# A modulation vector's sums over the partitions, 512 columns at once or four times 128

## The chip, the cores and the metric

The kernel runs on one core of a Trainium2 chip. The metric is the device time of one execution in microseconds; the number for a version is the median of its runs. Engines are named as in the profile: PE does matmuls (PEld loads their weights), DVE and ACT do elementwise work, POOL (GpSimd) issues DMAs and a few operations of its own, SP issues DMAs only.

## What is computed

Two layers of a backbone over 512 latent tokens and 256 context tokens, with 1024 features and in float32. A layer is a SwiGLU feed-forward part (FFN), a token mixer (a gMLP in layer 0, attention in layer 1) and a second FFN. Each of these six parts is modulated by three vectors, a shift, a scale and a gate, that come from a conditioning vector:

```python
def modulation(cond, w_mod, b_mod):
    m = jax.nn.silu(cond) @ w_mod + b_mod
    return jnp.split(m[..., None, :], N_MOD, axis=-1)

def ffn_sublayer(x, shift, scale, gate, w_in, w_out, ln_g, ln_b):
    y = swiglu(modulate(x, shift, scale), w_in, w_out)
    return layer_norm(ALPHA * x + 0.5 * gate * y, ln_g, ln_b)
...
        m_lat = modulation(c, w_mod[i], b_mod[i])
        m_ctx = modulation(c_ctx, w_mod[i], b_mod[i])
```

There are two conditionings, one for the latent tokens and one for the context, and nine vectors of 1024 per layer. The products of `silu(cond)` with `w_mod` (1024 x 9216 per layer) are what this case is about.

## The kernel before

Each float32 operand of a matmul is split into a high part (a cast on ACT) and a low part (a subtraction on DVE), and each product is made of three matmuls. So ACT and DVE prepare every tile of weights (`raw`, loaded by SP, becomes `w`) and every tile of activations that PE uses.

An FFN has two phases. The in-projection multiplies by the first weight matrix (in a form with fewer products, with sums and differences of weight tiles on DVE) and stores most of the resulting activations in DRAM: `act<-stage`, a DMA that POOL issues (line 90 is a helper that issues for many). The out-projection then goes twice over 22 pieces of activations, once per half of 512 output columns. In step x it multiplies piece x for six blocks of 128 tokens, 18 matmuls, while piece x+3 is prepared: POOL issues the load `q<-act` from DRAM (two DMAs of 384 columns per piece, into six buffers `q`), ACT casts `acts<-q`, DVE makes the low part `acts<-q,acts`. At the change of halves DVE takes the six finished banks out of PSUM (`q<-ps,gate`), which must have begun before PE can reuse the first.

The modulation vectors are made beside all this, without PE. `mod_unit` (lines 453 to 483) makes one vector in two halves of 512 columns. For each half it goes over eight blocks of 128 rows of `w_mod`: SP loads a block into `mraw` (three buffers), and DVE multiplies it by the conditioning's value of each row and adds it to `acc`, once per conditioning (two for all vectors up to (1, 4), one after that). After eight blocks each of the 128 partitions of `acc` holds a partial result for each of the 512 columns. Line 476 sums over the partitions, on POOL, with the result in every partition, and line 477 adds partition 0 to the vector in DRAM (`mod`, where the bias stands already) by a DMA that POOL issues too. Two of the 18 vectors are made by PE at the start, and 16 are left to this code: 12 with two conditionings and 4 with one, in two halves each, which makes 56 sums.

The units are cut into steps by `yield`; `fill` and `fill_pair` take the next step in slots that the phases offer. DVE, ACT, PE, SP and the DMAs of POOL keep the order in which the program was written in these phases (the class `Pinned`). Line 476 calls POOL directly and not through `Pinned`, so a scheduler may place the sums. Each engine works its own queue in order, so that what stands behind a sum in POOL's queue waits for it.

Of the kernel before, what the change touches and what calls it, by code (L numbers as in the profile page):

```python
# [13 lines left out]
P = 128  # L14
# [80 lines left out]
class Backbone:  # L95
# [357 lines left out]
    def mod_unit(self, l, i):  # L453

        nc, io = self.nc, self.io
        nconds = self.nconds(l, i)
        m = self.mods[l, i] = self.dram.tile([2, D], F32, name=f"mod{l}{i}")
        for c in range(nconds):
            self.pool.dma_start(m[c : c + 1, :], io["b_mod"][l, i * D : i * D + D].unsqueeze(0))
        for half in range(2):  # L460
            accs = [self.acc() for _ in range(nconds)]
            for k in range(KD):
                raw, dve = self.next_raw(), self.dve
                self.light = nconds == 1
                for c in range(nconds):
                    cs = self.cs[:, c * KD + k : c * KD + k + 1]
                    if k:
                        dve.scalar_tensor_tensor(accs[c], raw, cs, accs[c], ALU.mult, ALU.add)
                    else:
                        dve.tensor_scalar(accs[c], raw, cs, None, ALU.mult)  # L470
                self.filler_raw()
                if k < KD - 1:
                    yield
            s = slice(half * 512, half * 512 + 512)
            for c in range(nconds):
                nc.gpsimd.partition_all_reduce(accs[c], accs[c], P, bass_isa.ReduceOp.add)  # L476
                nc.gpsimd.dma_start(m[c : c + 1, s], accs[c][0:1, :], accum_op=ALU.add)
            yield
        self.mod_sent.add((l, i))
        if i % 3 == 2:  # L480
            self.mod_done.add((l, i))
        elif {(l, i - i % 3), (l, i - i % 3 + 1)} <= self.mod_sent:
            self.later(READ_LATER, lambda: self.mod_columns(l, i - i % 3))
# [1870 lines left out]
```

## Time and profile before

| | |
|---|---|
| median of 3 runs | 2781.74 us (2780.76 to 2783.99) |
| the profiled execution | 2782.34 us |
| its span in the profile | 2780.6 us |
| mean clock granted to PE | 0.996 of full speed |
| idle time of PE in the span | 51.8 us |
| sums of line 476: count, busy time | 56, 206.6 us |
| DMAs of line 477: count, busy time on POOL | 56, 46.9 us |
| `q<-act` loads: count of DMAs, busy time on POOL | 234, 132.2 us |
| read from and written to HBM | 383.40 and 64.19 MB |

An engine's share of the span is its busy time, whatever it waits for next. POOL's busy time for a sum runs from its issue, so it includes what a sum waits for once it has been issued. In the chain of waits each row is what the next one waited for last. A DMA's row on POOL is the issue; the transfer comes after it. A group's name reads out<-in; `x2` at the end of a timeline's row is two instructions merged into it.

### The profile page before, as it was taken

Reading aid. Unit: us, or ns where it says so; the run is one execution under the profiler, and the core shown is the slowest. Engines: PE = TensorE matmul, PEld = TensorE weight load, DVE = VectorE, ACT = ScalarE, POOL = GpSimd, SP = SyncE. Lnnn points to the kernel's source line nnn. Section 1 sums busy time; section 2 is a strip of 40 time slices with the busy share of each in tenths; the row PEclk is TensorE's granted clock in tenths of the full one; section 3 lists DMA queues with packets and bytes.
Section 4 is the critical chain, followed back from the end, with each engine's and each line's share of the span. In section 5 each row is a group of like instructions: output and inputs, shape, how many; then the busy total and the mean of one; then the engine's idle time right before and its main releaser. Section 6 shows DMA issues by size and latency. Waiting matters only on the chain.

```text
span 2780.6 us, 40722 instructions
## 1 busy us (share of the span) xinstructions
PE 2728.8 (98%) x14234; PEld 2460.8 (89%) x14234; DVE 2082.2 (75%) x3554; ACT 1314.7 (47%) x2624; POOL 554.4 (20%) x627
## 2 busy tenths in 40 slices
PE   7999999999999999999999999999999999999998
PEld 5999987888899988899998889999888888888887
DVE  6879989587789876687998659789795698733445
ACT  6644432475666632554444246444432666623321
POOL 1003144212122233100314120013242121000001
PEclk9999999999999999999999999999999999999999
DMA  7444566367656674344547434445594424354352
GB/s 235 133 140 139 147 221 220 104 212 234 199 180 196 191 265 146 114 149 142 143 139 240 158 107 145 144 143 145 179 304 144 144 76 100 125 149 132 109 169 87
DMA packets 408134, 448.09 MB, mean 161 GB/s; under 512 B 29624, under 2 KB 289144, under 8 KB 407928
## 3 DMA queue, kind: packets, MB, share of 16 engines
q1 hardware_dynamic: 371416, 331.99, 38.3%
q0 software_dynamic: 36512, 113.51, 13.4%
q8 instruction: 111, 1.82, 0.3%
q14 instruction: 95, 0.78, 0.1%
HBM read 383.40 MB, written 64.19 MB: 161 GB/s over the span
## 4 chain that ended last, share of the span: by engine, by line
PE 77%; DVE 7%; issue 5%; DMA 4%; ACT 4%; POOL 2%; SPq 0%; DVEq 0%; ACTq 0%; POOLq 0%
PE ps L90 77%; DVE w L90 1%; DMA mraw<-in_w_mod_dram 1%; DVE acc L90 1%; POOL acc L476 1%; PE pp L90 1%; ACT w L90 1%; DMA raw<-in_w_mod_dram 1%; DMA q<-act 1%; DMA acc<-in_gmlp_w_in_dram 1%; DMA raw<-in_gmlp_w_in_dram 1%; ACT h L694 1%; ACT z L2252 0%; POOL q L90 0%; DVE z L90 0%
## 5 line engine op out<-in xcount | busy, mean ns | idle before, releaser
L90 PE MATMUL ps<-comb,w 128*128 128x384 f32 x6552 | 1153.6, 336 | 6.5 <-DVE w L90 2.5
L90 PEld LDWEIGHTS ps<-comb,w 128*128 128x128 f32 x6552 | 1139.1, 189 | 10.1 <-DVE w L90 3.8
L90 PE MATMUL ps<-w,acts 128*128 128x512 f32 (+1 forms) x3792 | 861.6, 389 | 5.3 <-DVE q L90 4.8
L90 PEld LDWEIGHTS ps<-w,acts 128*128 128x128 f32 x3792 | 707.2, 188 | 151.6 <-DVE q L90 6.1
L90 ACT CAST w<-raw 128x512 fp32r<-128x512 f32 x643 | 397.5, 621 | 627.7 <-PE ps L90 535.3
L90 DVE TENSOR_TENSOR w<-raw,w 128x512 fp32r<-128x512 f32 x643 | 474.7, 743 | 283.1 <-ACT w L90 281.7
L90 DVE SCALAR_TENSOR_TENSOR acc<-mraw,cs,acc 128x512 f32<-128x512 f32 x392 | 279.1, 745 | 24.7 <-DMA mraw<-in_w_mod_dram 24.5
L476 POOL PARTITION_ALL_REDUCE acc<-acc x56 | 206.6, 3697 | 324.3 <-DVE acc L90 297.1
L90 PE MATMUL ps<-h,w 128*128 128x512 f32 (+1 forms) x1152 | 241.4, 372 | 0.2 <-DVE w L174 0.2
L90 PEld LDWEIGHTS ps<-h,w 128*128 128x128 f32 x1152 | 203.3, 188 | 37.7 <-DVE w L174 0.4
L90 POOL DMA_DIRECT2D act<-stage x86 | 48.5, 564 | 902.5 <-DVE stage L90 840.1
L90 ACT COPY q<-ps 128x384 f32<-128x384 f32 (+1 forms) x218 | 104.3, 481 | 238.0 <-PE ps L90 237.9
L90 POOL DMA_DIRECT2D q<-act x234 | 132.2, 601 | 419.5 <-DVE acts L90 278.6
L90 DVE TENSOR_TENSOR w<-sums,w 128x512 fp32r<-128x512 f32 x234 | 165.1, 712 | 45.3 <-ACT w L90 45.1
L90 PE MATMUL ps<-w,comb 128*128 128x512 f32 x756 | 173.7, 391 | 0.5 <-DVE w L90 0.2
L90 PEld LDWEIGHTS ps<-w,comb 128*128 128x128 f32 x756 | 141.4, 188 | 31.5 <-DVE w L90 1.0
L90 ACT CAST w<-sums 128x512 fp32r<-128x512 f32 x234 | 145.1, 621 | 50.9 <-DVE sums L355 29.3
L90 ACT CAST acts<-q 128x384 fp32r<-128x384 f32 (+1 forms) x272 | 132.1, 519 | 73.9 <-DMA q<-act 55.2
L90 DVE TENSOR_TENSOR acts<-q,acts 128x384 fp32r<-128x384 f32 (+1 forms) x272 | 153.6, 602 | 11.1 <-ACT acts L90 11.0
L204 POOL TENSOR_TENSOR rs<-ve,mhalf 128x1 f32<-128x1 f32 (+3 forms) x47 | 38.6, 820 | 274.5 <-DVE ve L201 170.7
L90 DVE TENSOR_TENSOR q<-q,ps 128x384 f32<-128x384 f32 (+1 forms) x81 | 46.2, 570 | 57.9 <-PE ps L90 57.9
L174 DVE TENSOR_TENSOR w<-raw,w 128x512 fp32r<-128x512 f32 x101 | 67.2, 689 | 26.7 <-ACT w L173 26.2
(203 smaller groups left out, 2485.6 us busy)
## 6 DMA issues: line engine op xcount, KB each, us to landing
raw<-in_ffn_w_in_dram SPq DMA_DIRECT2D x400, 256.0 KB
mraw<-in_w_mod_dram SPq DMA_DIRECT2D x256, 256.0 KB
raw<-in_ffn_w_out_dram SPq DMA_DIRECT2D x176, 256.0 KB
q<-act POOLq DMA_DIRECT2D x224, 192.0 KB, 4.3
raw<-in_gmlp_w_in_dram SPq DMA_DIRECT2D x132, 256.0 KB
act<-stage POOLq DMA_DIRECT2D x76, 384.0 KB, 3.2
zhat<-z POOLq DMA_DIRECT2D x26, 512.0 KB, 3.0
raw<-in_gmlp_w_out_dram SPq DMA_DIRECT2D x48, 256.0 KB
```

The lines of the kernel that those rows point to most:

```text
L90: return self.tc.keep_in_program_order(f(*args, **kwargs))
L174: self.lows.append((key, lambda: self.dve.tensor_tensor(lo, src, hi.bitcast(F32), ALU.subtract)))
L204: self.last_rstd = self.nc.gpsimd.tensor_tensor(rs, ve, self.mhalf[:, 0:1].to_broadcast([P, n]), ALU.pow).ins
L476: nc.gpsimd.partition_all_reduce(accs[c], accs[c], P, bass_isa.ReduceOp.add)
L694: self.act.activation(h32[:, kk], ps[:, s], AF.Identity, bias=bi, scale=sc)
```

## The change

The sum of 512 columns becomes four sums of 128 columns, one after another on POOL, over consecutive parts of the same tile. The DMA to `mod` behind them is as before and takes all 512 columns.

```diff
             for c in range(nconds):
-                nc.gpsimd.partition_all_reduce(accs[c], accs[c], P, bass_isa.ReduceOp.add)
+                for x in range(4):
+                    part = accs[c][:, x * P : x * P + P]
+                    nc.gpsimd.partition_all_reduce(part, part, P, bass_isa.ReduceOp.add)
                 nc.gpsimd.dma_start(m[c : c + 1, s], accs[c][0:1, :], accum_op=ALU.add)
```

The order of the instructions of PE, DVE, ACT and SP is the same in both kernels. On POOL the 56 sums become 224. The rows of POOL's queue in the first half of the first out-projection, before (a DMA `q<-act_7` loads stored piece 7; `mod_3862` is vector 4 of layer 0; an `ISA` row with `acc` is a sum, line 476 before and 478 now):

```order
L90 DMA q<-act_5_969 128x384 x2
L90 DMA q<-act_6_970 128x384 x2
L476 ISA acc<-acc 128x512
L477 DMA mod_3862<-acc 16x1x32
L476 ISA acc<-acc 128x512
L477 DMA mod_3862<-acc 16x1x32
L90 DMA q<-act_7_971 128x384 x2
L90 DMA q<-act_8_972 128x384 x2
```

And now, at the same place:

```order
L90 DMA q<-act_5_969 128x384 x2
L90 DMA q<-act_6_970 128x384 x2
L478 ISA acc<-acc 128x128 x4
L479 DMA mod_3886<-acc 16x1x32
L478 ISA acc<-acc 128x128 x4
L479 DMA mod_3886<-acc 16x1x32
L90 DMA q<-act_7_971 128x384 x2
L90 DMA q<-act_8_972 128x384 x2
```

The loads of pieces 7 and 8 stand behind eight short sums instead of two long ones; nothing else has moved. In the in-projections and in the gMLP both sums of a pair stood ahead of both DMAs at some places. One of them, in the gMLP, before:

```order
L90 DMA act_13_7176<-stage 128x768
L476 ISA acc<-acc 128x512 x2
L477 DMA mod_7638<-acc 16x1x32 x2
L90 DMA mod_8691<-in_b_mod_dram 16x64 x2
L90 DMA act_14_7177<-stage 128x768
```

And now:

```order
L90 DMA act_13_7224<-stage 128x768
L478 ISA acc<-acc 128x128 x5
L479 DMA mod_7686<-acc 16x1x32
L478 ISA acc<-acc 128x128 x3
L479 DMA mod_7686<-acc 16x1x32
L90 DMA mod_8751<-in_b_mod_dram 16x64 x2
L90 DMA act_14_7225<-stage 128x768
```

Here the first conditioning's DMA now stands behind the fifth short sum, ahead of the last three of the second conditioning. There are five such places.

## The prediction

> **What bounds the kernel now.** I read the busy shares first, then a table of stretches, then what PE waits for.
>
> ```profile
> PE 2728.8 (98%) x14234; PEld 2460.8 (89%) x14234; DVE 2082.2 (75%) x3554; ACT 1314.7 (47%) x2624; POOL 554.4 (20%) x627
> ```
>
> PE is busy in 98% of the span, so all that anything else can give back is 52 us, and POOL, where the change is, works a fifth of the time. An edit on POOL costs or gains only where POOL's lateness, or what POOL takes from DVE, reaches PE. The table of stretches says where PE is not full: the columns are length, busy time with count for PE, PEld, DVE, ACT and POOL, granted clock, DMA share, GB/s.
>
> ```profile
> 60.00:360.00 300.00, 298.72 (x1726) 298.05 (x1727) 254.51 (x413) 152.03 (x305) 37.76 (x34) 1.00 0.47 138
> 360.00:470.00 110.00, 108.08 (x495) 91.19 (x494) 97.37 (x141) 38.28 (x76) 58.54 (x56) 1.00 0.70 240
> 1500.00:1590.00 90.00, 90.00 (x398) 74.28 (x397) 64.33 (x107) 26.11 (x52) 23.00 (x31) 1.00 0.60 201
> 1980.00:2090.00 110.00, 107.11 (x485) 89.44 (x484) 91.19 (x148) 39.23 (x76) 42.76 (x49) 1.00 0.84 280
> ```
>
> The first row is an FFN's in-projection: sums run there too, yet PE idles 1.3 us in 300, and not for them. The second and fourth are first halves of out-projections, with DVE at 89% and 83% of their 110 us; the third is such a half with DVE at 71% and no idle PE at all. The table of PE's waits, asked of 360 to 470 us, of 2080 to 2090, and of 870 to 890 in the gMLP (two rows), gives:
>
> ```profile
> PE ps L90 <- DVE q L90: 1.9, 1, 1.9
> PE ps L90 <- DVE q L90: 0.3, 1, 0.3
> PE ps L90 <- DVE q L90: 1.7, 1, 1.7
> PE ps L90 <- DVE S L90: 0.4, 1, 0.4
> ```
>
> Small sums, but a PE that waits for DVE has no reserve left: whatever makes DVE later before that point is paid in full. The chain of waits (start, length, what) back from PE's 1.9 us wait, which ended at 467.10, is this:
>
> ```profile
> 412.36 4.44 DMA q<-act
> 428.61 5.21 POOL acc L476
> 434.93 3.21 POOL acc L476
> 441.70 4.09 DMA q<-act
> 466.36 0.69 DVE q L90
> 467.10 3.02 PE ps L90 x12
> ```
>
> The sums (line 476) stand in it, and behind each pair the load of the next stored activations, `q<-act`. POOL's own timeline at the pair before (start, length, instruction) shows why:
>
> ```profile
> 400.44 1.08 POOL L90 DMA_DIRECT2D q<-act  x2 [11.27 <-DVE acts L90]
> 401.56 5.02 POOL L476 PARTITION_ALL_REDUCE acc<-acc  x1
> 406.87 0.83 POOL L477 DMA_DIRECT2D mod<-acc  x1 [0.30 <-POOL acc L476]
> 407.48 3.45 POOL L476 PARTITION_ALL_REDUCE acc<-acc  x1
> 411.22 0.80 POOL L477 DMA_DIRECT2D mod<-acc  x1 [0.30 <-POOL acc L476]
> 411.77 1.93 POOL L90 DMA_DIRECT2D q<-act  x3
> ```
>
> POOL issues no load from 401.5 to 411.8, because two sums and their two DMAs stand ahead in its queue. ACT, DVE and PE need those activations in turn. **So the first half of the first out-projection (360 to 470 us) is where a longer sum costs time.**
>
> **The change part by part.** Removed are 56 sums of 512 columns, added 224 of 128; no other engine's order changes, and no new wait stands anywhere but POOL.
>
> *One piece.* What a sum takes, by the groups of the page and by the answer for its line (min/median/max in ns):
>
> ```profile
> L476 POOL PARTITION_ALL_REDUCE acc<-acc x56 | 206.6, 3697 | 324.3 <-DVE acc L90 297.1
> L476 POOL PARTITION_ALL_REDUCE acc<-acc x56: 3223/3473/5366, 221.2 to 2598.4; - x56
> ```
>
> 3.22 us is one sum with nothing in its way; the mean is 0.47 us longer. No sum of another width is in the trace, so the fixed part F of the 3.22 us is bounded from both sides. With F, four pieces take 3.22 + 3F. Near the low end stand POOL's other instructions:
>
> ```profile
> L90 POOL TENSOR_TENSOR z<-z,rows 128x512 f32<-128x512 f32 x4 | 6.2, 1562 | 2.4 <-ACT z L2297 2.2
> L90 POOL TENSOR_TENSOR z<-z,rows 128x256 f32<-128x256 f32 x2 | 1.5, 731 | 1.0 <-ACT z L2297 0.9
> L2341 POOL MEMSET const-float32-0.0<- 128x1 f32 x1 | 0.1, 98 | 0.2 <-issue 0.2
> ```
>
> Halving the columns halves the time (731 against 1562), and one column takes 98 ns: F as small as 0.1 us. The high end comes from a sum seen beside DVE, the third row being the same DVE operation undisturbed:
>
> ```profile
> 2118.01 3.23 POOL L476 PARTITION_ALL_REDUCE acc<-acc  x1 [5.43 <-DVE acc L90]
> 2118.37 2.42 DVE L90 TENSOR_TENSOR w<-raw,w 128x512 fp32r<-128x512 f32 x1 [0.46 <-ACT w L90]
> 1525.53 0.69 DVE L90 TENSOR_TENSOR w<-raw,w 128x512 fp32r<-128x512 f32 x1 [1.08 <-ACT w L90]
> ```
>
> DVE's operation lasts 2.42 us instead of 0.69, ends at 2120.79, and so really began at 2120.10: it was held for 2.1 us of the sum and released 1.13 us before the sum's end at 2121.24. I read the 2.1 us as the sum's reading and the 1.13 us as what follows the last read. If all of that is a lag that every piece pays, F is 1.13 us. A sum across partitions has reading that grows with the columns and a tail that need not, and neither row is nearer to it, so I take the middle, F = 0.6: a piece takes 0.6 + 2.62/4 = 1.26 us and the four 5.0, which is **1.8 us more per sum**. To that comes a fresh chance for DVE to slip in ahead of pieces two to four: between nothing and the mean excess of 0.47 us each. The second sum of the pair above shows 3.45 - 3.22 = 0.23; three times that is 0.7. So **POOL is busy X = 2.5 us longer per sum** (ends 0.3 and 1.13 x 3 + 0.47 x 3 = 4.8).
>
> *What DVE loses.* Now 1.7 us in the row above. In pieces, DVE is held in each piece's reading and runs in its tail. The readings add up to the same 2.1 us and a start or two: Y = +0.4 us per sum is my value, with ends -0.8 (DVE gets through in every tail) and +2.
>
> [...]
>
> *First out-projection.* Four sums (the pairs at 401 and 428 us) stand in the chain as POOL work ahead of a load: 4X = 10.0. The third pair (456 to 465 us) acts through DVE: 2Y = 0.8. Both are paid in full at the wait that ends at 467: **+10.8**. The two pairs' ends are 1.2 and 19.2, the third's -1.6 and +4.
>
> *The last first half (layer 1).* One condition less, so single sums; its chain is:
>
> ```profile
> 2027.67 3.60 POOL acc L476
> 2032.69 5.88 DMA q<-act
> 2045.53 3.60 POOL acc L476
> 2052.67 5.08 DMA q<-act
> 2059.51 8.71 DMA mraw<-in_w_mod_dram
> ```
>
> Two sums would give 2X = 5.0, but the chain then hangs on a fetch of 8.71 us in a stretch with the DMA engines at 0.84. Later loads leave that queue emptier, so I let half through: **+2.5** (ends 0 and 9.6).
>
> *gMLP.* The pairs at 871 and 920 us are followed by PE waits for what DVE makes (1.7 and 0.4 us after the first). Four sums at Y are 1.6, of which I take **+1.0** (ends -2 and +5).
>
> *What is hidden.* In-projections: POOL only stores there, and PE kept its 298.7 of 300 us. Out-projections of the other layers, at the pair that starts at 1511.82:
>
> ```profile
> 1520.49 3.54 POOL L90 DMA_DIRECT2D q<-act  x6
> 1526.14 1.02 DVE L90 TENSOR_TENSOR acts<-q,acts 128x384 fp32r<-128x384 f32 x2
> 1558.77 1.02 DVE L90 TENSOR_TENSOR acts<-q,acts 128x384 fp32r<-128x384 f32 x2
> 1572.34 3.08 DVE L90 SCALAR_TENSOR_TENSOR q<-ps,gate 128x512 f32<-128x512 f32 x5
> ```
>
> From the second row to the third are eight activations at 4.08 us, PE's pace. The third finishes the half's last one at 1559.8; PE ends the half at 1572.3 and takes 4.08 us over each, so it starts on that one at 1568.3. That is a lead of 8.5 us against a delay of 2X = 5.0: nothing reaches PE. Past X = 4.2 it would.
>
> Sum: 10.8 + 2.5 + 1.0 = 14.3 us on the profiled execution's 2782.3, which lies 0.6 above the median of 2781.7: **2796.6, rounded to 2796.5 us**.
>
> **The rivals.** *Nothing to measure (2780 to 2787).* Pieces might follow one another without paying F: one begins while the last is in its tail. Then X is near 0.3 to 1.0 and the sum is 1 to 5 us: 2785.
>
> ```profile
> 821.44 7.10 POOL L476 PARTITION_ALL_REDUCE acc<-acc  x2 [6.78 <-DVE S L90]
> ```
>
> Against it: two sums back to back took 7.10 us, above 2 x 3.22 = 6.45, so no overlap shows; DVE's interference may have covered it, though. For it: the 98 ns row. [...] The same times result if POOL's lateness is absorbed by loads that were early after all. Chance 0.27.
>
> *Faster (2775.4).* DVE gets through between the pieces and its own lateness goes. The places are 456 to 467 us, 871 to 883 us and 2069 to 2086 us, and the price is all of PE's waits there: 1.9 + 0.3 + 1.7 + 0.4 = 4.3 us, and 2.6 more if what PE waits for after 920 us goes likewise: 6.9. It decides from the point where four pieces hold DVE for under the 1.7 us of now while POOL grows by less than 0.5 us per sum (4X < 2). For it: DVE is released before a sum's end. Against: loads wait for the whole of a sum, not for its reading. Chance 0.05.
>
> *Much slower (2806 to 2822).* F is 1.13 and each piece waits 0.47: X = 4.8 gives 19.2 + 2Y in the first stretch, half of 9.6 in the last and the gMLP's share; with Y = 1, 19.2 + 2 + 4.8 + 4 = 30 us, 2812, and the lead of 8.5 us above is used up as well. Chance 0.13.
>
> That the change does not do what it says would need pieces out of order; POOL's order shows all 224 ahead of their DMAs, so it gets no chance of its own.
>
> **How the numbers follow.** The forecast (2788 to 2806) has 0.55. The bound of what can be told from no change is 0.2%, 5.6 us: slower is 0.55 + 0.13 = 0.68, within it 0.27, faster 0.05. The range of 2782 to 2814 leaves out the faster case, the low edge of the rival near nothing and the top of the slow one, some 0.15.
>
> **What would show it.** A piece of 128 columns near 1.26 us undisturbed (0.9 is the first rival, 1.65 the slow one); the gap between `q<-act` loads around 401 us grown from 10.3 to about 15 us; PE's wait at the end of that half 12 us rather than 1.9, or spread over earlier waits for `acts`; DVE's operations held several times by about half a microsecond instead of once by two. The forecast is wrong if the gap grows and PE does not wait (absorbed), or if the gap does not grow (pieces cheap).

## The result, and the profile after

| | before | after |
|---|---|---|
| median of 9 runs each (us) | 2783.68 (2780.76 to 2787.35) | 2775.84 (2774.03 to 2777.82) |
| ratio | | 0.9976 (95%: 0.9967 to 0.9985) |
| span of the profiled execution (us) | 2780.6 | 2774.7 |
| busy time of DVE (us) | 2082.2 | 2037.6 |
| busy time of POOL (us) | 554.4 | 637.0 |

The kernel became faster by 0.24%, 4 to 9 us. The forecast of 2796.5 us was wrong: the time of the rival that I had given 0.05, at 2775.4, is what came, though only in part from the places that it named. The row of busy times after:

```profile
PE 2726.2 (98%) x14234; PEld 2457.6 (89%) x14234; DVE 2037.6 (73%) x3554; ACT 1315.3 (47%) x2624; POOL 637.0 (23%) x795
```

POOL works 82.6 us longer, as a longer sum should make it. But DVE works 44.6 us less, with the same 3554 instructions: 44.6 / 56 = 0.80 us less per sum. The groups say what a piece costs, and the line's answer has the spread (min/median/max in ns):

```profile
L478 POOL PARTITION_ALL_REDUCE acc<-acc x224 | 291.9, 1375 | 320.4 <-DVE acc L90 293.3
```

```profile
L478 POOL PARTITION_ALL_REDUCE acc<-acc x224: 1062/1302/3205, 219.5 to 2595.6; - x112
```

An undisturbed piece takes 1.06 us, so four take 4.25 where one sum takes 3.22, and F = 1.03 / 3 = 0.34 us. By the groups, POOL is busy 291.9 - 206.6 = 85.3 us more for the sums, X = 1.5 us each. POOL's timeline at the pair that the prediction showed:

```profile
398.69 1.08 POOL L90 DMA_DIRECT2D q<-act  x2 [11.28 <-DVE acts L90]
399.80 6.92 POOL L478 PARTITION_ALL_REDUCE acc<-acc  x4
407.02 0.83 POOL L479 DMA_DIRECT2D mod<-acc  x1 [0.30 <-POOL acc L478]
407.62 5.13 POOL L478 PARTITION_ALL_REDUCE acc<-acc  x4
413.05 0.80 POOL L479 DMA_DIRECT2D mod<-acc  x1 [0.30 <-POOL acc L478]
413.60 2.99 POOL L90 DMA_DIRECT2D q<-act  x5
```

From the end of the first loads (399.77) to the next (413.60) it is now 13.8 us instead of 10.3. The first sum takes 6.92 instead of 5.02, X = 1.9, and the second 5.13 instead of 3.45, X = 1.7. So the lateness that I had forecast is there, at two thirds of its size. PE's waits from 360 to 470 us after:

```profile
PE ps L90 <- ACT acts L90: 1.0, 2, 0.7
PE ps L90 <- DVE q L90: 0.5, 1, 0.5
```

There were 1.9 us before, there are 1.5 now, and not the 12 that I expected. So where did the gain come from? I cut the program at four places that can be found in each profile, and compared the lengths: the first FFN (from the last `modT` operation of the start, at 60.4 us before, to the first store of `zhat`, at 540.5) is 480.1 us before and 480.7 after, the stretch from the gMLP to the attention (from 961.0 to the first `nm` at 2256.9) 1295.9 and 1296.7. Only the gMLP's is much shorter. Its ends are the first and the last of 48 operations of DVE on the spatial product, in the answer for the tile `S` (min/median/max in ns, then the start of the first and the last), before and after:

```profile
L90 DVE SCALAR_TENSOR_TENSOR S<-ps,sguT,s x48: 601/610/620, 752.9 to 961.0; 128x384 f32<-128x384 f32 x48
```

```profile
L90 DVE SCALAR_TENSOR_TENSOR S<-ps,sguT,s x48: 600/614/629, 752.1 to 954.0; 128x384 f32<-128x384 f32 x48
```

208.1 us have become 201.9. That is 6.2 us, where the two spans differ by 5.9 in all. What PE waited for from 860 to 965 us, before and then after:

```profile
PE ps L90 <- ACT v L90: 1.8, 1, 1.8
PE ps L90 <- DVE q L90: 1.7, 1, 1.7
PE ps L90 <- DVE S L90: 1.2, 2, 0.8
PE ps L90 <- ACT q L90: 0.5, 1, 0.5
```

```profile
PE ps L90 <- DVE S L90: 1.4, 1, 1.4
PE ps L90 <- ACT q L90: 0.5, 1, 0.5
```

5.2 us have become 1.9. DVE's timeline at the pair of sums around 871 us shows what changed for DVE. Before (the sums run from 870.80 to 879.53):

```profile
872.98 3.47 DVE L90 TENSOR_SCALAR acc<-mraw,cs 128x512 f32<-128x512 f32 x2
876.36 0.27 DVE L90 COPY S<-ps 128x128 f32<-128x128 f32 x1
876.56 2.52 DVE L90 TENSOR_TENSOR w<-raw,w 128x512 fp32r<-128x512 f32 x1
879.00 0.68 DVE L355 TENSOR_TENSOR sums<-raw,sums 128x512 f32<-128x512 f32 x1
```

After (five pieces from 869.17 to 877.22, three from 877.67 to 881.58):

```profile
871.35 1.30 DVE L90 TENSOR_SCALAR acc<-mraw,cs 128x512 f32<-128x512 f32 x2
872.58 0.27 DVE L90 COPY S<-ps 128x128 f32<-128x128 f32 x1
872.77 0.80 DVE L90 TENSOR_TENSOR w<-raw,w 128x512 fp32r<-128x512 f32 x1
...
877.70 1.29 DVE L336 TENSOR_TENSOR sums<-raw 128x512 f32<-128x512 f32 x1 [1.75 <-DMA raw<-in_gmlp_w_in_dram]
878.91 0.68 DVE L90 TENSOR_TENSOR w<-raw,w 128x512 fp32r<-128x512 f32 x1
879.51 1.00 DVE L347 TENSOR_TENSOR raw<-raw 128x512 f32<-128x512 f32 x1
```

The same operations lose 3.47 - 1.30 = 2.2 and 2.52 - 0.69 = 1.8 us before, one for each sum. After, 0.11 at the `w`, 0.6 at the `sums`, 0.3 at the `raw`: some pieces hold DVE for a fraction of their own length, the others not at all. A sum waits for DVE too. The first of the pair, before, and the first piece, after:

```profile
870.80 5.37 POOL L476 PARTITION_ALL_REDUCE acc<-acc  x1
```

```profile
869.17 3.21 POOL L478 PARTITION_ALL_REDUCE acc<-acc  x1
```

Both take 2.15 us more than alone (3.22 and 1.06), while DVE works off several operations in a row, the last of which ends at 873.07 and 871.44. I read that as a wait for DVE; here it is paid once by the sum, not once by each piece.

### The profile page after: what moved, and what is told of

Its sections match the earlier page's. It is cut to its first block, busy times and chain, and to the rows that moved or that the text cites. A ratio compares the mean times of both kernels' runs of the same rounds, so it can differ in the third digit from the quotient of the medians.

```text
span 2774.7 us, 40890 instructions
## 1 busy us (share of the span) xinstructions
PE 2726.2 (98%) x14234; PEld 2457.6 (89%) x14234; DVE 2037.6 (73%) x3554; ACT 1315.3 (47%) x2624; POOL 637.0 (23%) x795
## 4 chain that ended last, share of the span: by engine, by line
PE 81%; issue 5%; DVE 4%; ACT 4%; POOL 3%; DMA 3%; SPq 0%; DVEq 0%; POOLq 0%; ACTq 0%
PE ps L90 80%; POOL acc L478 2%; PE pp L90 1%; DVE w L90 1%; DMA q<-act 1%; DMA raw<-in_w_mod_dram 1%; ACT h L696 1%; ACT z L2254 0%; DVE acc L90 0%; ACT w L173 0%; DMA acc<-in_gmlp_w_in_dram 0%; DVE q L90 0%; DVE w L174 0%; POOL q L90 0%; ACT p L1768 0%
## 5 line engine op out<-in xcount | busy, mean ns | idle before, releaser
L90 DVE TENSOR_TENSOR w<-raw,w 128x512 fp32r<-128x512 f32 x643 | 449.8, 705 | 289.4 <-ACT w L90 288.1
L478 POOL PARTITION_ALL_REDUCE acc<-acc x224 | 291.9, 1375 | 320.4 <-DVE acc L90 293.3
L90 DVE SCALAR_TENSOR_TENSOR acc<-mraw,cs,acc 128x512 f32<-128x512 f32 x392 | 285.2, 761 | 26.1 <-DMA mraw<-in_w_mod_dram 25.8
L90 ACT CAST acts<-q 128x384 fp32r<-128x384 f32 (+1 forms) x272 | 132.8, 519 | 82.6 <-DMA q<-act 64.8
L174 DVE TENSOR_TENSOR w<-raw,w 128x512 fp32r<-128x512 f32 x101 | 67.3, 688 | 24.1 <-ACT w L173 23.6
```

Source lines behind the costliest of these rows:

```text
L90: return self.tc.keep_in_program_order(f(*args, **kwargs))
L174: self.lows.append((key, lambda: self.dve.tensor_tensor(lo, src, hi.bitcast(F32), ALU.subtract)))
L478: nc.gpsimd.partition_all_reduce(part, part, P, bass_isa.ReduceOp.add)
```

## The experiments

Each kernel was timed beside the kernel before on the same chip, and a ratio is to those runs. The theory after the result (Theory A in the expectations) was: **the gain is DVE's shorter holds in the gMLP; POOL's lateness costs little, because it reaches PE only at one place.** Its rivals: the gain comes from everywhere, DVE being freer in all stages; POOL's later work, or the DMA of the first conditioning that now stands among the pieces, moves something in the gMLP that helps by accident.

**Where: four pieces in the gMLP alone (vectors 6 to 8 of layer 0), and everywhere else.** The first as a diff against before, with `1 if ... else 4` for the second:

```diff
-                nc.gpsimd.partition_all_reduce(accs[c], accs[c], P, bass_isa.ReduceOp.add)
+                n = 4 if l == 0 and i >= 6 else 1
+                for x in range(n):
+                    part = accs[c][:, x * 512 // n : (x + 1) * 512 // n]
+                    nc.gpsimd.partition_all_reduce(part, part, P, bass_isa.ReduceOp.add)
```

> Only the 12 sums of the three vectors made during the gMLP (layer 0, vectors 6 to 8) are done in four pieces, the other 44 whole. Theory A (a sum holds up DVE; pieces hold it up for less; that matters only in the gMLP, where PE waits for DVE and its granted clock then drops to half for some 5 us): nearly the whole gain, 2776 to 2779 us against 2783, PE's waits between 870 and 940 us down from 4.7 us to under 2, no row with a clock under 0.9 there. Theory B (POOL's later timing at all sums, or many small gains everywhere): a fifth of the gain, about 2782.

> The complement: the 44 sums outside the gMLP in four pieces, the 12 in the gMLP whole. Theory A: 2782 to 2785 us, no gain, PE waiting in the gMLP and losing its clock there as before. Theory B: about 2777. My forecast's term for the first out-projection (POOL's loads later by 4X, paid in full) would show here alone: 2790 or more.

Measured: in the gMLP alone 2777.86 against 2783.27 us, 0.9982 (0.9974 to 0.9991); everywhere else 2782.07, 0.9997 (0.9988 to 1.0005). Twelve of the 56 sums bring all of the gain that can be told; the other 44 bring none (the interval leaves room for 0.12%), though they free 2082.2 - 2042.6 = 39.6 us of DVE, 0.9 us per sum. That removes the rival "everywhere". PE's waits from 860 to 965 us in these two, the gMLP alone first:

```profile
PE ps L90 <- DVE q L90: 1.7, 1, 1.7
PE ps L90 <- DVE S L90: 1.5, 1, 1.5
PE ps L90 <- ACT q L90: 0.5, 1, 0.5
```

```profile
PE ps L90 <- DVE S L90: 2.0, 2, 1.2
PE ps L90 <- DVE q L90: 1.7, 1, 1.7
PE ps L90 <- ACT v L90: 1.6, 1, 1.6
PE ps L90 <- ACT q L90: 0.5, 1, 0.5
```

With pieces in the gMLP alone, unlike in the full change, the 1.7 us for `q` stayed and the wait for ACT's `v` went; 3.2 us are left where I had expected under 2. Why it was this wait that stayed was not measured.

**Width: two pieces of 256, eight of 64.** The same edit with `n = 2` and `n = 8`.

> All sums as two of 256 columns. With a fixed part of 0.34 us a piece alone takes about 1.78 us and a sum 3.56. Theory A: DVE is held for about 1.0 us at a time instead of 2.1, two holds a sum; between the two kernels, 2776 to 2781. If the fixed part of a piece were what matters, it would be better than four pieces.

> All sums as eight of 64 columns. A piece alone about 0.70 us, a sum 5.6 us, POOL about 1.5 us longer per sum than with four. Theory A: DVE's holds no longer than with four, the gMLP as good: 2774 to 2779 unless POOL's lateness now reaches PE in the first out-projection. The forecast's POOL theory: slower than four pieces by 4 us or more, 2780 or above.

Measured: 2778.47, 0.9982 (0.9974 to 0.9991), and 2777.71, 0.9981 (0.9972 to 0.999). The answers for the line of the sum (479 in these kernels), 256 columns and then 64:

```profile
L479 POOL PARTITION_ALL_REDUCE acc<-acc x112: 1782/2023/3924, 221.5 to 2598.3; - x112
```

```profile
L479 POOL PARTITION_ALL_REDUCE acc<-acc x448: 703/792/3060, 220.3 to 2597.7; - x150
```

With 3.22 and 1.06 this is a line of 5.6 ns per column and 0.34 us fixed. DVE's busy time falls with the width: 2082.2, 2068.1, 2037.6, 1997.0 us for 512, 256, 128 and 64 columns. With eight pieces the gMLP is shorter still (200.3 us), but the first FFN longer (485.3 instead of 480.1), and its wait is the one that I had feared. PE's waits from 360 to 470 us with 64 columns:

```profile
PE ps L90 <- ACT acts L90: 4.3, 1, 4.3
```

The loads stand behind longer pairs, so ACT's `acts` come late, and PE waits; its clock is 0.55 and 0.77 in the two slices of 5 us from 420 us on. The forecast's mechanism exists; with 128 columns for all sums it hardly shows in the time (the vectors taken one by one, below, say why).

**How much there is to gain in the gMLP: its 12 sums left out.** This leaves out the sums over the partitions of vectors 6 to 8 of layer 0; their DMAs stay.

```diff
-                nc.gpsimd.partition_all_reduce(accs[c], accs[c], P, bass_isa.ReduceOp.add)
+                if l or i < 6:
+                    nc.gpsimd.partition_all_reduce(accs[c], accs[c], P, bass_isa.ReduceOp.add)
```

> The 12 sums in the gMLP are left out (the DMA sends partition 0's partial result, so layer 0's last three modulation vectors are not the reference's); all else as before. It bounds what sums cost there. Theory A: nothing holds DVE, so the gMLP takes 200 us or less and the time is 2774 to 2777. If holds were not the cause (order of the DMAs, clock by chance), 206 to 208 us and 2781 or more.

Measured: 2777.07 against 2782.15, 0.9983 (0.9974 to 0.9992). Of PE's waits from 860 to 965 us one is left:

```profile
PE ps L90 <- ACT q L90: 0.5, 1, 0.5
```

DVE is busy 2065.5 us, 16.7 less than before, 16.7 / 12 = 1.4 us per sum (I had taken 1.7). But only six of the 12 sums (the pairs at 821, 871 and 920 us) fall between the first and the last operation on the spatial product. The others, at 987 to 1102 us, run in a stretch where PE has nothing to get back: it is busy 130.00 of the 130 us from 980 on. The row of busy times from the first to the last of those operations, before and without the 12 sums (length, then busy time with count of PE, PEld, DVE, ACT and POOL, clock, DMA share, GB/s):

```profile
752.90:961.00 208.10, 202.49 (x1223) 198.84 (x1223) 182.57 (x318) 133.93 (x308) 46.28 (x45) 0.98 0.60 187
```

```profile
750.20:950.60 200.40, 199.41 (x1223) 196.37 (x1223) 170.35 (x317) 134.33 (x308) 23.02 (x39) 1.00 0.62 194
```

There a whole sum costs DVE (182.57 - 170.35) / 6 = 2.0 us. Without any sum the gMLP takes 200.4 us (I had expected 200 or less); four pieces come within 1.5 to 3.2 us of that.

**POOL's lateness without pieces: three memsets behind each whole sum of the gMLP** (over rows of `acc` that nobody reads).

```diff
+                if l == 0 and i >= 6:
+                    for x in range(3):
+                        nc.gpsimd.memset(accs[c][64:96, :], 0.0)
```

> Whole sums as before; in the gMLP alone three memsets of 512 columns follow each sum on POOL (some 1.5 us, into rows 64 to 95 of the tile, which nothing reads after the sum), so that POOL stays longer, as with pieces, but reads nothing more. Theory A (what counts is how long DVE is held by a sum's reading): as before, 2781 to 2786, the gMLP 207 to 210 us. Rival (POOL being later shifts work out of each other's way): the gMLP near 204 us, 2777 to 2779.

Measured: 2782.58, 1.0002 (0.9993 to 1.0011). POOL is 2.0 us later per sum (36 memsets, 24.0 us), more than pieces make it, and nothing is gained or lost. One reservation: at the pairs at 822 and 872 us both sums ran ahead of the memsets, so only the DMAs and what follows them came later there; at 921 us the second sum was delayed too.

**The moved DMA: pieces in the gMLP, with both DMAs issued behind both conditionings there.**

```diff
+            mixing = l == 0 and i >= 6
...
+                if not mixing:
+                    send(c)
+            for c in range(nconds if mixing else 0):
+                send(c)
```

> Four pieces in the gMLP alone, as in the first experiment, but both conditionings' DMAs behind all eight pieces, as they stood before the change, so that the moved DMA is undone. Theory A: no difference to the first experiment, gMLP 202 to 205 us, 2776 to 2779. Rival (the earlier DMA of the first conditioning is the gain): 207 us or more, 2781 to 2784.

Measured: 2775.24, 0.9979 (0.997 to 0.9988), a little under my range, with the gMLP at 202.1 us. The DMA's place is not the cause. With the memsets this removes the second rival, as far as their reservation lets it.

**One table for the gMLP.** From the profiled executions, PE's waits from 860 to 965 us, DVE's busy time in the stage (the same operations in each, as in the two rows above) and the length of the stage:

| sums in the gMLP | kernels | PE waits (us) | DVE busy (us) | gMLP (us) |
|---|---|---|---|---|
| whole | before; all but the gMLP; padded; vector 4 only; vector 5 only | 5.2; 5.8; 4.9; 4.8; 4.7 | 182.6; 182.2; 183.1; 182.3; 182.0 | 208.1; 208.1; 206.8; 204.9; 206.4 |
| two of 256 | two pieces | 4.2 | 179.6 | 205.1 |
| four of 128 | after; gMLP only; DMAs behind; after again | 1.9; 3.7; 0.9; 1.0 | 176.7; 176.5; 175.9; 177.0 | 201.9; 203.6; 202.1; 202.2 |
| eight of 64 | eight; mixed; mixed again | 0.5; 0.5; 0.5 | 171.9; 171.7; 171.7 | 200.3; 201.8; 200.3 |
| none | left out | 0.5 | 170.4 | 200.4 |

Whole sums mean 206.9 us, four pieces 202.5: **the gMLP's share of the gain is 4.4 us**. Of these, 3.2 are PE's waits (5.1 and 1.9 on average). The other 1.2 stand in PE's busy time, 201.3 and 200.0 us on average for the same 1223 matmuls, and go with the granted clock, 0.98 in the first row above and 1.00 in the second (last section). DVE's busy time above that without sums, by the six sums in the stage, is 2.0 us per sum when they are whole, 1.0 in four pieces and 0.2 in eight.

**Why the first FFN pays nothing: vector 4 alone, vector 5 alone.** The two pairs at 401 and 428 us belong to vector (0, 4), the third at 457 to (0, 5). The edit is `n = 4 if (l, i) == (0, 4) else 1`, and `(0, 5)`.

> Only vector 4 of layer 0 in four pieces: the two pairs of sums near 401 and 428 us that stand ahead of loads; the third pair (vector 5, 456 to 465 us) and all others whole. Theory A with DVE's recovery (the later loads cost, but DVE, held for less, catches up, and the rest is paid back by the third pair's shorter holds): PE's waits in the first half of the first out-projection 3 to 5 us instead of 1.9, the half ending 407 to 409 us after the last of the start's modulation columns instead of 406.0. My forecast's term with the measured X of about 1.7 (4X, paid in full): 8 to 9 us of waits, 412 to 413.

> The complement in that stretch: vector 5 alone in four pieces, so that only the third pair changes before the half ends. Theory A: DVE is held 1.5 to 2 us less there, PE's wait of 1.9 us falls under 0.5, the half ends after 404.0 to 404.8 us. My forecast's term (2Y = +0.8): a wait of 2.7 us, 406.8.

Measured: vector 4 alone **2788.67** against 2782.87 us, 1.0023 (1.0014 to 1.0032), slower; vector 5 alone 2781.41, 0.9993 (0.9984 to 1.0002). With vector 4 alone, PE waits from 360 to 470 us for:

```profile
PE ps L90 <- DVE q L90: 3.5, 1, 3.5
PE ps L90 <- ACT acts L90: 1.0, 2, 0.6
```

With vector 5 alone it waits for nothing there. The first FFN takes 485.4 and 477.9 us, 5.3 more and 2.2 less than with whole sums (480.1); with both vectors in pieces it took 480.7, 480.1 and 480.8 us in three kernels, against 479.9 to 480.4 in five with whole sums: hardly anything is to be seen. The loads come late in the half, and the third pair, right before its end, gives the time back to DVE. Before, the second sum of that pair holds an operation of 0.17 us; with vector 5 in pieces the same one runs free:

```profile
461.04 2.78 DVE L644 TENSOR_TENSOR modB<-modB,modT 128x16 f32<-128x16 f32 x1
```

```profile
457.57 0.17 DVE L647 TENSOR_TENSOR modB<-modB,modT 128x16 f32<-128x16 f32 x1
```

PE's lengths do not add up: -2.2 and +5.3 make 3.1. DVE's nearly do. Its first operation at the change of halves starts 406.0 us after the last `modT` operation of the start before, 409.7 with vector 4 alone, 401.8 with vector 5 alone (I had expected 407 to 409 and 404.0 to 404.8), and 406.5 and 406.7 with both. So vector 5 makes DVE 4.2 us earlier, of which PE can use only the 1.9 that it waited; the rest is room for the 3.7 us by which vector 4 makes DVE later.

**A faster version, and the change once more.** 64 columns everywhere but for vectors 4 and 5 of layer 0, which have two pieces of 256: `n = 2 if l == 0 and i in (4, 5) else 8`. Run twice, the second time beside the change itself.

> Eight sums of 64 columns for all vectors, but two of 256 for vectors 4 and 5 of layer 0, whose sums fall into the first out-projection. Theory A with POOL's lateness as a second, local cost: the gMLP as short as with 64 columns everywhere (about 200 us between its first and last spatial product, against 208 before and 202 with 128), no wait of PE for loaded activations in the first out-projection (4.3 us and a clock drop with 64 everywhere), so 2770 to 2774 us, below both kernels. If narrower sums gained nothing more, 2775 to 2778.

> The mixed version (64 columns, but 256 for vectors 4 and 5 of layer 0) beside the changed kernel: 0.9960 to 0.9975 of before, 1 to 4 us under the changed kernel, if shorter holds in the gMLP and ahead of the last layer's out-projection are worth what its first profile shows.

> The changed kernel once more, for a comparison on the same chip with the next one: 0.9976 of before by its first measurement; 0.9970 to 0.9983 now.

Measured: 2773.63, 0.997 (0.996 to 0.998), then 2772.88, 0.9964 (0.995 to 0.9978); the change beside the second 2778.52, 0.9982 (0.9973 to 0.999). So the mixed one has the lowest medians of all kernels here, 10 us under before in the second group (8.5 in the first) and 5.6 under the change (I had expected 1 to 4), though the intervals of the two still overlap. In the gMLP its waits are those of no sums (table above), and the 4.3 us for `acts` from 360 to 470 us are gone: PE waits 1.8 us for DVE there in the second run. From 1975 to 2095 us, in the last first half, PE's waits in the second run are

```profile
PE ps L90 <- DVE q L90: 0.4, 1, 0.4
```

against 2.9 before; in the first run of the same kernel they were 2.8, so I don't count that place as shown. Eight pieces everywhere had 0.5 there, though, and the stage from the gMLP to the attention took 1292.8, 1295.4 and 1292.8 us in the three profiled executions with 64 columns in it, against 1295.1 to 1297.2 with 128. So a good part of what the mixed version has over the change probably comes from there; it was not measured alone.

## Why the prediction was wrong, step by step

Two steps failed: what DVE loses got the wrong sign (Y), and POOL's lateness at the first out-projection, 10.0 of the 14.3 us, was taken as paid in full by PE.

- **One piece (F = 0.6, 1.26 us).** F measured 0.34 and the piece 1.06: mis-sized, inside its bounds.
- **X = 2.5 us.** Measured 1.5 on average, and 1.9 and 1.7 at the pair at 401 us. At its second sum the fixed parts are 3 x 0.34 = 1.03, and the other 0.65 is close to the 0.7 that I had added for waits between pieces.
- **What DVE loses, Y = +0.4: the step that gave the wrong sign.** Measured -0.80 on average (in the gMLP -1.0: a sum costs DVE 1.0 us there instead of 2.0), the end that I had called "DVE gets through in every tail". I had added up the readings of four pieces and let DVE wait for them all. But as the rows at 871 us read, an operation of DVE that meets a sum is held until shortly before that one instruction's end (I read it as the end of its reading; the second sum's row ends at 879.53, and the `w` that it held began at 879.08 - 0.69 = 878.39), and then goes, ahead of the next piece. That is some 2 us at a whole sum, and from nothing to 0.6 at a piece. The shorter the piece the less: -0.25 us per sum with 256 columns, -0.80 with 128, -1.52 with 64 (from the busy times above, by 56).
- **Whose turn it is.** Whether DVE and POOL take turns, one instruction each, was not shown. Pieces with a median 0.24 us above their minimum (1.30 and 1.06 us) agree with it; that both first sums at 871 us took 2.15 us more than alone while DVE worked off several operations in a row does not look like a turn after each. Nor did a whole sum hold DVE to its end: the `w` at 2118 us went on 1.13 us before it, the one at 876 us 1.14 us.
- **First out-projection, +10.8: the step that gave the size.** The stage is unchanged (+0.7 in the profiled executions). The term 4X was right in kind: vector 4 in pieces by itself costs 5.3 us there and makes the kernel slower. But it is not paid in full: with X at 1.9 and 1.7, POOL loses some 7 us at the two pairs, of which 3.7 reach DVE's end of the half. The term 2Y has the wrong sign: vector 5 by itself gives PE 2.2 us and DVE 4.2. That the pieces of the first two pairs free DVE too (0.9 us per sum on average outside the gMLP, an estimate of 3.6 for four) would close the gap between 7 and 3.7; it was not measured apart.
- **The last first half, +2.5.** PE waits 2.8 us there instead of 2.9: nothing. I had asked for its waits from 2080 us alone, which gave 0.3, though the row of that stretch shows 2.9 idle; the other 2.6 end at 1997, ahead of both sums in my chain, and stay. The stage from the gMLP to the attention took 1296.7, 1297.2 and 1295.1 us in three kernels with four pieces there, and 1295.7 to 1298.0 in seven with whole sums.
- **gMLP, +1.0.** Measured -4.4. The wrong sign of Y, at the place where PE hangs on DVE and on nothing that POOL loads.
- **What is hidden.** Nothing speaks against it: pieces everywhere but in the gMLP give 0.9997.
- **The rival "faster"** named the gMLP and PE's waits of 1.7, 0.4 and 2.6 us as its price, and was right there (4.7 us, and 4.4 came). That the whole, 6.9 us, also comes near is luck: the 1.9 and 0.3 us that it took at the other two places did not come. Its condition was wrong: I let it decide only while POOL grows by under 0.5 us per sum. POOL grew by three times that, and no harm came in the gMLP.

Together: -4.4 in the gMLP, and differences in the other stages that lie within their spread between executions, against a measured -6.7 (-4.2 to -9.2, the ratio on 2783.7). The 2.3 us between them lie inside that interval and have no place of their own.

## What to carry to other kernels

Ask of a long instruction whether another engine's operations wait for it. Here a whole sum cost DVE some 2 us in the gMLP; cut into four it cost 1.0, into eight 0.2, and the fixed price of the pieces (0.34 us for each further one here) is worth paying where the other engine sets the pace and the pieces' own engine does not. Look for both kinds of place in the same profile: here pieces helped where PE waited for DVE (4.4 us in the gMLP), and hurt where PE's loads stood behind them in POOL's queue (5.3 us in the first FFN with vector 4 alone), so the best width differed by place. And when a cost depends on who comes when, its bounds are not a dress around a middle value: both signs were open, and the chance of the lower one should have been more than 0.05.

## What the runs showed of the hardware

The granted clock was lower right behind some of PE's short waits (0.50 and 0.66 of full speed in the slices of 5 us named here), so that such a wait may have cost more than its length. The stretches before, at the end of the gMLP (length, busy time with count of PE, PEld, DVE, ACT and POOL, clock, DMA share, GB/s):

```profile
930.00:935.00 5.00, 2.65 (x15) 1.97 (x13) 5.00 (x12) 2.91 (x7) 2.50 (x5) 0.93 0.98 310
935.00:940.00 5.00, 4.81 (x17) 4.84 (x18) 5.00 (x11) 2.08 (x5) 0.00 (x0) 0.50 0.88 304
940.00:945.00 5.00, 5.00 (x28) 5.00 (x27) 4.90 (x10) 2.42 (x6) 0.55 (x1) 0.89 0.33 93
```

The same place after:

```profile
930.00:935.00 5.00, 4.02 (x25) 4.05 (x26) 5.00 (x10) 2.07 (x5) 2.62 (x5) 1.00 0.67 219
935.00:940.00 5.00, 5.00 (x31) 5.00 (x30) 4.90 (x11) 4.47 (x12) 0.11 (x1) 1.00 0.75 279
```

Before, PE waited 1.8 and 0.8 us here and then had a mean clock of 0.50 over 5 us: 5.0 x (0.07 + 0.50 + 0.11) = 3.4 us of full-speed work at most lost on top of 2.6. So up to 6 us hung on 2.6 us of waits in this execution. What lowers the clock, and behind how long a wait, was not shown. It varies between executions: of the five with whole sums there, two, the longest, have such a slice behind these waits (all but the gMLP in pieces: 0.66 behind 1.6 and 0.8 us), and three have none (1.00 behind 1.4 to 1.5 and 0.8 us). The gMLP's whole sums range from 204.9 to 208.1 us. Slices of 0.66 to 0.94 also stand at the very start of the stage, with whole sums and with pieces, so not all of the 1.2 us above is the change's. Vector 4 alone shows a slice of 0.66 right behind its 3.5 us, 1.7 of the 5.3 us that it costs. My price for a wait was its length alone.

Two pieces one behind the other overlap by 0.09 us and no more: in the single rows of POOL's timeline the first piece at 869.17 ends at 872.38, and the next begins at 872.29. Rows of DVE that follow one another overlap by as much (872.58 + 0.27 = 872.85 against 872.77), so no piece is seen to begin while another is in its tail.
